# Two fixed tiles for the decay matrices, and a planner that knows transfers queue

## The chip, the cores and the metric

The kernel is one program on one NeuronCore of a Trainium2 chip. Five engines take part: TensorE (PE; its weight loads are listed as PEld), VectorE (DVE), ScalarE (ACT), GpSimd (POOL) and SyncE (SP), which does no arithmetic and issues every DMA of this program. The metric is device time in microseconds of one execution. Before the change the median of three runs is 2250.44 us (2250.43 to 2253.73). A program on one core has a single span; "clock" below is the share of TensorE's clock that the throttle granted, as the trace records it.

## What is computed

A two-layer decoder trunk on 1024 positions of width 1024, float32. Layer 0 is attention and a gated linear recurrence; the change does not touch it. Layer 1, the "odd layer", is a gated DeltaNet with 16 value heads that share 8 key heads. Cut to what matters:

```python
qkv, z, b_logit, a_logit = split(rms_norm(h) @ w_in)
q, k, v = split(silu(causal_conv4(qkv)));  q, k = l2_normalize(q), l2_normalize(k)
decay = exp(where(causal, gcum[:, None] - gcum[None, :], -inf))      # per head and chunk
lower = where(strict, (k*beta) @ k.T * decay, 0)
u, w  = triangular_solve(lower + I, [v*beta, k*beta*exp(gcum)])
step:   v_new = u - w @ S;  o = (q*exp(gcum)) @ S + (q @ k.T * decay) @ v_new
        S = S * exp(g_last) + k_tail.T @ v_new
out = h + (rms_norm(o) * silu(z)) @ w_out
```

followed by a final RMSNorm. `gcum` is the running sum of the log decay within a chunk.

## The kernel before, in words

**Tiling.** The odd layer works on 8 key heads `hh`, each with its two value heads `e`, and on 8 chunks `c` of 128 positions. Head `hh` goes through four kinds of work:

- *Projections* with short convolutions (`proj`, `conv`, `way_out`): float32 products split into three single-pass matmuls of 128x512 (`pk`, `pv`, `pq`, `oz` in the trace). They are most of TensorE's work and depend on nothing of the recurrence. Their weights come through `raww` tiles, which ACT and DVE cut into `w_hi` and `w_lo`.
- *Inversion* (`invert(hh)`): tile `L`, 16 blocks of 128x128, blocks 2c and 2c+1 for chunk c. `decays` loads the running sums of one chunk from the DRAM tile `gcd`, 128 KB for two blocks; ACT turns them into decays (a Relu per block with bias `g_ngc`, an Exp for four blocks); TensorE forms k k^T into the PSUM tile `kk` (four chunks a tile, so `kk{hh}_0` and `kk{hh}_1`, in one bank "c"); DVE multiplies it onto `L`. A long chain on DVE inverts 32x32 triangles, and three rounds of short matmuls join them (`qp` and `up`, 32x32, then `q2`/`u2`, 64x64). The result overwrites `L` and is called `U`.
- *Recurrence* (`recur(hh)`), chunk after chunk: `ks` and `qs` (state times k and q), `vp` (which reads U of this chunk), `kv`, `op`. The causal part needs a tile `A` per chunk, also loaded from `gcd` (128 KB), masked by POOL, passed through Exp on ACT and multiplied by `qk` on DVE.
- *Output* (`normed`, `gated`): POOL scales, TensorE transposes (`ot`), the result goes to DRAM.

**What runs beside what.** While `recur(hh)` runs, `invert(hh+1)`, the projections of head hh+1 and the output of head hh-1 are recorded as its filler. So the L of head hh+1 is needed at the start of stage hh, right where `recur(hh-1)` has just finished.

**What sets the order.** Nothing of the odd layer is issued when the Python code reaches it. `Plan` records all 8709 operations, finds their dependencies by overlapping elements (`edges`), and `run` sets them out in time by a list schedule: again and again it takes the engine that can start soonest and, of its operations that are ready, the one recorded earliest. `times` (line 119) says how long an operation holds its engine and when its result is there; it is a table of constants, for a DMA 430 ns of SP and 3100 ns to the landing, whatever else is in flight. `give` (line 291) then issues everything in the order of the planned starts, and each engine works strictly in that order. Hence nearly all instructions of this layer have line L291 in the profile, and groups are told apart by tile.

**Tiles that rotate.** `L` comes from a pool tag "L" with two buffers: a new tile takes the place of the tile before last, and both the planner (the "gates" in `edges`) and the framework make the first use of the new tile wait for *every* use of the old. The L of head hh+1 takes the buffer of head hh-1, which is read until the last `vp` of `recur(hh-1)`. The same tag also serves `gtmp` at the start of the layer and `g7` at its end. One operation waits for more than its data: the tile framework orders accesses to one PSUM tile, so a matmul into `kk` that stands behind a DVE read of the same tile in the issued order waits for that read.

Of the kernel before, what the change touches and what calls it, by code (L numbers as in the profile page):

```python
# [10 lines left out]
F32 = mybir.dt.float32  # L11
# [8 lines left out]
P = 128  # L20
D = 1024
T = 1024
NT = T // P
# [58 lines left out]
class Plan:  # L82
# [33 lines left out]
    def elems(ap):  # L116
        return int(np.prod([n for _, n in ap.ap[1:]], dtype=np.int64))

    def times(self, op, last):

        key, name, a, out = op["key"], op["name"], op["a"], op["out"][0]
        n = self.elems(out)
        if key == "SP":
            return 430, 3100
        if key == "PE":
            if name == "transpose":
                return 109, 290
            r32 = a[1].dtype == F32R
            rows, cols = a[2].ap[0][1], self.elems(a[1])
            small = rows < 128 or cols < 128  # L130
            if small:
                held = 28 if cols == 32 else 62
            else:
                held = n / 2.4 * (1 if r32 else 4) + (17 if r32 else 8)
            if small != last.get("small", False):
                held += 100
            last["small"] = small
            return held, held + 190
        if key == "DVE":
            if name == "transpose":  # L140
                t = 1980 if n >= 1024 else 1060 if out.ap[-1][0] != 1 or a[1].ap[-1][0] != 1 else 95 + 1.03 * n
            elif name == "memset":
                t = 60 + 0.86 * n
            elif n < 24:
                t = 82
            elif out.ap[0][1] == 32:
                t = 715
            elif n >= 512:
                t = (65 if name == "scalar_tensor_tensor" and len(op["ins"]) == 3 else 12) + 1.155 * n
            elif name == "scalar_tensor_tensor":  # L150
                t = 260
            else:
                t = 72 + 1.03 * n
            return t, t + 83
        if key == "ACT":
            if n < 24:
                t = 200
            elif op["ins"][0].space == PSUM:
                t = 249 if n <= 128 else 268 if n <= 256 else 0.93 * n
            else:  # L160
                t = 293 if n <= 128 else 307 if n <= 256 else 1.02 * n
            if n >= 512 and (len(op["ins"]) > 1 or out.ap[0][1] == 32):
                t += 100
            return t, t + (230 if "accum_out" in op["kw"] else 110)
        if name == "memset":
            return 565, 565
        t = 750 if n <= 256 or out.ap[0][1] == 32 else 1010 if len(op["ins"][1].ap) > 2 else 1250
        return t, t + 50
# [55 lines left out]
    def run(self):  # L224
        ops = self.ops
        pred, gates = self.dag = self.edges()
        n = len(ops)
        succ = [[] for _ in range(n + len(gates))]
        deg = [0] * (n + len(gates))
        for i, ps in enumerate(pred):  # L230
            for j in ps:
                succ[j].append(i)
                deg[i] += 1
        for g, (old, new, _) in enumerate(gates):
            inner = set(new)
            for j in old:
                succ[j].append(n + g)
                deg[n + g] += 1
            for i in new:
                if not pred[i] & inner:  # L240
                    succ[n + g].append(i)
                    deg[i] += 1
        keys = ("PE", "DVE", "ACT", "POOL", "SP")
        ready = {k: [] for k in keys}
        free = {k: 0.0 for k in keys}
        at = [0.0] * (n + len(gates))

        def release(j, done, key):
            for i in succ[j]:
                k = ops[i]["key"] if i < n else None  # L250
                if k is None:
                    t = done
                else:
                    t = 0.0 if k == key == "PE" else done + (self.OWN if k == key else self.SEM[k])
                at[i] = max(at[i], t)
                deg[i] -= 1
                if not deg[i]:
                    if i < n:
                        ready[k].append(i)
                    else:  # L260
                        release(i, at[i], None)

        for i in range(n):
            if not deg[i]:
                ready[ops[i]["key"]].append(i)
        last, starts, done_n, ends = {}, [0.0] * n, 0, [0.0] * n
        while done_n < n:
            best = None
            for k in keys:
                if ready[k]:  # L270
                    s = max(free[k], min(at[i] for i in ready[k]))
                    if best is None or s < best[0]:
                        best = s, k
            if best is None:
                raise RuntimeError("the order of the tiles' places does not work out")
            s, k = best
            i = min((i for i in ready[k] if at[i] <= s), key=lambda i: ops[i]["want"])
            ready[k].remove(i)
            held, got = self.times(ops[i], last)
            starts[i] = s  # L280
            free[k] = s + held
            ends[i] = s + got
            release(i, s + got, k)
            done_n += 1
        self.starts, self.ends = starts, ends
# [26 lines left out]
def trunk_kernel(ctx: ExitStack, tc: tile.TileContext, x, ew, ewo, ow, owab, owo, nw, fnw, lbl, hnw,  # L312
# [148 lines left out]
    def ab_half(w, half):  # L461

        w = w.rearrange("p (k j) -> p k j", k=KC)
        p = bank("pj", [P, 512], f"abp{half}")
        s = slice(half * 512, half * 512 + 512)
        for k in range(2):
            for r in range(4):
                for part in ("hi", "lo"):
                    pe.matmul(p[32 * r:32 * r + 32], w[:, 2 * r + k], hn(part, 2 * r + k, s).bitcast(F32),
                              start=k == 0 and part == "hi", stop=k == 1 and part == "lo")  # L470
        return p
# [605 lines left out]
    def odd_layer(es):  # L1077
        plan.ops = []
        sp = es.enter_context(tc.tile_pool(name="od", bufs=1))
        gt = {n: sp.tile([P, NT, 16], F32, name=f"g_{n}") for n in ("beta", "gc", "ngc", "eg", "nbeg", "etl", "egl")}  # L1080
        MA = sp.tile([P, 128], F32, name="MA")
        sync.dma_start(MA, cst[:, C_MA:C_MA + 128])
        cws = sp.tile([P, 32, 4], F32, name="cws")
# [5 lines left out]
        def gates():  # L1089
# [12 lines left out]
            for half in range(2):  # L1102
                p = begun.pop(("ab", half), None) or ab_half(w, half)
                s = slice(half * 512, half * 512 + 512)
# [6 lines left out]
            yield 3, 1.6  # L1111
            act.activation(gt["beta"], tp[:, :, 0:16], AF.Sigmoid)

            tmp = sp.tile([P, 6, NT, 16], F32, name="gtmp", tag="L", bufs=2)
            a_, u, w_, l_, d_, g = (tmp[:, i] for i in range(6))
            dve.tensor_tensor(a_, tp[:, :, 16:32], dt[:, None, :].to_broadcast([P, NT, 16]), op=ALU.add)
            dve.scalar_tensor_tensor(u, a_, -1.0, a_, op0=ALU.mult, op1=ALU.max)
            act.activation(u, u, AF.Exp, scale=-1.0)
# [69 lines left out]
        def turn_q(j):  # L1188
            CQ[j] = sp.tile([P, NT], F32, name=f"cq{j}", tag="cq", bufs=3)
            ss = sp.tile([P, NT], F32, name=f"qss{j}", tag="qss", bufs=2)  # L1190
            turn_qk(Q[j], ss, f"tq{j}")
            dve.tensor_scalar(CQ[j], ss, 4.0 * EPS, 128.0 * EPS, op0=ALU.add, op1=ALU.mult)
# [64 lines left out]
        G7 = []  # L1257
# [36 lines left out]
                yield from gate(hh, w, e, lambda h, g: gated(hh, e, h, g))  # L1294

        def gate7():
            G7.append(sp.tile([P, 2, 2, 512], F32, name="g7", tag="L", bufs=2))
            turn_q(7)
            w = unit()
            for e in range(2):  # L1300
                yield from gate(7, w, e, lambda h, g: None)
# [13 lines left out]
        def invert(hh):  # L1315
            kT = KT[hh]

            L = sp.tile([P, 16, 128], F32, name=f"L{hh}", tag="L", bufs=2)
            Lg = sp.tile([P, 16, 32], F32, name=f"Lg{hh}", tag="Lg")

            for c in range(0, NT, 2):

                decays(L[:, 2 * c:2 * c + 2, :], hh, c)
                decays(L[:, 2 * c + 2:2 * c + 4, :], hh, c + 1)
                for u in range(4):
                    act.activation(L[:, 2 * c + u, :], L[:, 2 * c + u, :], AF.Relu,
                                   bias=gt["ngc"][:, c + u // 2, 2 * hh + u % 2:2 * hh + u % 2 + 1])
                act.activation(L[:, 2 * c:2 * c + 4, :], L[:, 2 * c:2 * c + 4, :], AF.Exp, scale=-1.0)
            for h in range(2):
# [18 lines left out]
            for k in range(31):  # L1348
                n = k // 2 + 1
# [66 lines left out]
        def recur(hh):  # L1416
# [4 lines left out]
            def decay_a(c):  # L1421
                DA = sp.tile([P, 2, 128], F32, name=f"A{hh}_{c}", tag="A", bufs=4)
                decays(DA, hh, c)
                pool.tensor_tensor(DA, DA, MA[:, None, :].to_broadcast([P, 2, 128]), op=ALU.add)
                for e in range(2):
# [126 lines left out]
    with ExitStack() as es:  # L1552
        odd_layer(es)
# [65 lines left out]
```

## Time and profile before

| what | value |
|---|---|
| runs, median | 2250.44 us |
| profiled execution, its own time | 2252.19 us |
| its span, first to last instruction | 2250.4 us |
| mean granted clock of TensorE | 0.982 |
| busy in the span | PE 96%, PEld 79%, DVE 63%, ACT 42%, POOL 11% |
| chain that ended last | PE 82%, DVE 7%, DMA 6%, ACT 2%, issue 2%, SPq 1% |
| odd layer in the span | about 1204 us to the end |

"Busy" counts arithmetic; a PE that waits shows as idle before the instruction that ends the wait, with the releaser behind an arrow. A PE at half clock still counts as busy, so lost clock has to be read from the column PEclk of a table by stretches. "Issue" is a wait for nothing that the profile can name. SPq is SP's queue: an entry there that lasts longer than the usual 0.3 to 0.4 us is a DMA instruction that itself had to wait.

### The profile page before, as it was taken

The numbers are of one execution on the slowest core, as the hardware profiler recorded it, in microseconds if no ns is written. First come the engines' busy times: TensorE is split into PE (matmuls) and PEld (weight loads), VectorE is DVE, ScalarE is ACT, GpSimd is POOL, SyncE is SP. The second block draws the span as 40 slices with busy tenths as digits, with TensorE's granted clock in tenths as the row PEclk, the third lists the DMA queues.
The fourth block names the chain that finished last, engine by engine and source line by source line (L and its number), as shares of the span: only waits on it lengthen the run. The fifth ranks groups of instructions, "written<-read, shape, count | busy, mean of one in ns | idle before, by whom it ended". The sixth has DMA issues, their size and how long they took to land.

```text
span 2250.4 us, 52461 instructions
## 1 busy us (share of the span) xinstructions
PE 2159.4 (96%) x21781; PEld 1776.3 (79%) x21781; DVE 1417.3 (63%) x3236; ACT 945.3 (42%) x2519; POOL 247.3 (11%) x252
## 2 busy tenths in 40 slices
PE   7999999999999999989999898989999999999998
PEld 6888888888887878757887687868787787887887
DVE  6353535453444444457677896968788787965677
ACT  6233333333232223222236755655565555553223
POOL 0010101010000000000000012221212121220100
PEclk9999999999999999989999999989999999999999
DMA  4111111114333334353233413231212323224223
GB/s 148 39 49 48 44 48 47 45 39 121 98 99 90 108 98 131 92 165 99 88 118 110 78 40 52 77 64 57 74 53 68 60 67 54 78 74 145 94 95 121
DMA packets 100079, 184.15 MB, mean 82 GB/s; under 512 B 12672, under 2 KB 30208, under 8 KB 99840
## 3 DMA queue, kind: packets, MB, share of 16 engines
q1 hardware_dynamic: 99840, 180.79, 27.9%
q8 instruction: 171, 2.80, 0.5%
q14 instruction: 68, 0.56, 0.1%
HBM read 151.25 MB, written 29.49 MB: 80 GB/s over the span
## 4 chain that ended last, share of the span: by engine, by line
PE 82%; DVE 7%; DMA 6%; ACT 2%; issue 2%; SPq 1%; POOL 0%; DVEq 0%; ACTq 0%; POOLq 0%
PE op L291 8%; PE op L305 7%; PE oz L291 7%; PE pv L291 6%; PE avp L305 4%; PE bq L305 4%; PE ak L305 4%; PE aq L305 4%; PE ag L305 4%; PE bf L305 4%; PE bip L305 4%; PE bg L305 3%; PE pk L291 3%; PE o L305 3%; PE S L305 3%; DMA L<-gcd 2%
## 5 line engine op out<-in xcount | busy, mean ns | idle before, releaser
L305 DVE TENSOR_TENSOR w_lo<-raww,w_hi 128x512 fp32r<-128x512 f32 x168 | 123.4, 738 | 151.3 <-ACT w_hi L305 150.7
L305 ACT CAST w_hi<-raww 128x512 fp32r<-128x512 f32 x168 | 104.3, 621 | 217.3 <-DMA raww<-in_ewo_dram 56.9
L291 PE MATMUL op<-w_hi,yplo 128*128 128x512 f32 x448 | 140.2, 391 | 0.7 <-DVE hr L291 0.7
L305 ACT ACTIVATE P<-P,nm 128x256 f32<-128x256 f32 (+7 forms) x128 | 71.4, 559 | 135.4 <-DVE nm L305 135.2
L291 DVE TENSOR_TENSOR hr<-hr,op 128x512 f32<-128x512 f32 x128 | 87.4, 686 | 47.4 <-PE op L291 44.9
L305 PE MATMUL op<-w_hi,yphi 128*128 128x512 f32 x320 | 104.7, 401 | 10.1 <-DVE hres L305 9.7
L291 ACT CAST w_hi<-raww 128x512 fp32r<-128x512 f32 x124 | 76.3, 615 | 84.3 <-DMA raww<-in_owo_dram 37.2
L291 PE MATMUL oz<-hn_hi,w_hi 128*128 128x512 f32 x256 | 111.6, 436 | 0.0
L291 PE MATMUL pv<-hn_hi,w_hi 128*128 128x512 f32 x256 | 108.9, 425 | 1.0 <-ACT uv L291 1.0
L291 POOL TENSOR_TENSOR A<-A,MA 128x256 f32<-128x256 f32 x64 | 57.3, 897 | 461.1 <-DMA A<-gcd 226.5
L291 PE MATMUL oz<-hn_lo,w_hi 128*128 128x512 f32 x256 | 105.3, 411 | 0.0
L291 PE MATMUL oz<-hn_hi,w_lo 128*128 128x512 f32 x256 | 104.5, 408 | 0.0
L291 PE MATMUL pv<-hn_lo,w_hi 128*128 128x512 f32 x256 | 104.4, 408 | 0.0
L291 PE MATMUL pv<-hn_hi,w_lo 128*128 128x512 f32 x256 | 102.4, 400 | 0.0
L291 DVE TENSOR_TENSOR w_lo<-raww,w_hi 128x512 fp32r<-128x512 f32 x124 | 91.7, 742 | 16.0 <-ACT w_hi L291 13.8
L305 DVE STREAM_TRANSPOSE PB<-P 128x256 f32<-128x256 f32 (+3 forms) x64 | 54.6, 853 | 73.1 <-ACT P L305 73.1
L291 PEld LDWEIGHTS op<-w_hi,yplo 128*128 128x128 f32 x448 | 84.1, 188 | 18.3 <-DVE hr L291 0.9
L291 PE MATMUL op<-w_lo,yplo 128*128 128x512 f32 x224 | 87.2, 389 | 0.0
L305 DVE TENSOR_TENSOR hres<-hres,op 128x512 f32<-128x512 f32 x96 | 64.8, 682 | 30.3 <-PE op L305 29.4
L305 PEld LDWEIGHTS op<-w_hi,yphi 128*128 128x128 f32 x320 | 61.1, 191 | 25.6 <-DVE hres L305 11.4
L305 DVE CUSTOM_DVE_ANT_0 P<-S,G 128x256 f32<-128x256 f32 (+7 forms) x128 | 58.1, 492 | 36.8 <-PE S L305 36.4
L305 POOL TENSOR_TENSOR ay<-ay,sg 128x512 f32<-128x512 f32 x16 | 20.1, 1278 | 498.6 <-DMA ay<-rdd 498.6
(355 smaller groups left out, 6406.4 us busy)
## 6 DMA issues: line engine op xcount, KB each, us to landing
raww<-in_ew_dram SPq DMA_DIRECT2D x128, 256.0 KB, 3.0
raww<-in_ow_dram SPq DMA_DIRECT2D x100, 256.0 KB, 3.0
V<-vd SPq DMA_DIRECT2D x64, 256.0 KB, 5.2
rawy<-ymix SPq DMA_DIRECT2D x64, 256.0 KB, 2.7
raww<-in_ewo_dram SPq DMA_DIRECT2D x32, 256.0 KB, 3.0
L<-gcd SPq DMA_DIRECT2D x64, 128.0 KB, 9.4
A<-gcd SPq DMA_DIRECT2D x64, 128.0 KB, 2.9
ymix<-oy SPq DMA_DIRECT2D x32, 256.0 KB, 2.3
```

The costliest lines, as they stand in the source:

```text
L291: ops[i]["f"](*ops[i]["a"], **ops[i]["kw"])
L305: return f(*a, **kw)
```

## The change

Three things, all in the odd layer.

1. `L` no longer rotates. `LL` holds two fixed tiles of the same size for the whole layer; head hh uses `LL[hh % 2]`, `gtmp` becomes six blocks of `LL[1]`, and `g7` all of `LL[0]`. With no new tile there is no wait for a whole old one: each load of a chunk depends on the operations that touch the same elements, the last of them the `vp` of that chunk two heads earlier.
2. The planner's time to the landing of a DMA becomes the larger of 3000 ns and what brings it to 1250 ns behind the last planned landing.
3. `run` passes the start time to `times` and keeps the last planned landing.

The operations, their number and their sizes stay the same; the order in which the engines get them changes, since the planner decides it.

```diff
--- before.py
+++ after.py
@@ -116,12 +116,12 @@
     def elems(ap):
         return int(np.prod([n for _, n in ap.ap[1:]], dtype=np.int64))
 
-    def times(self, op, last):
+    def times(self, op, last, at=0.0):
 
         key, name, a, out = op["key"], op["name"], op["a"], op["out"][0]
         n = self.elems(out)
         if key == "SP":
-            return 430, 3100
+            return 430, max(3000, last.get("landed", 0) + 1250 - at)
         if key == "PE":
             if name == "transpose":
                 return 109, 290
@@ -276,7 +276,9 @@
             s, k = best
             i = min((i for i in ready[k] if at[i] <= s), key=lambda i: ops[i]["want"])
             ready[k].remove(i)
-            held, got = self.times(ops[i], last)
+            held, got = self.times(ops[i], last, s)
+            if k == "SP":
+                last["landed"] = s + got
             starts[i] = s
             free[k] = s + held
             ends[i] = s + got
@@ -1078,6 +1080,8 @@
         plan.ops = []
         sp = es.enter_context(tc.tile_pool(name="od", bufs=1))
         gt = {n: sp.tile([P, NT, 16], F32, name=f"g_{n}") for n in ("beta", "gc", "ngc", "eg", "nbeg", "etl", "egl")}
+
+        LL = [sp.tile([P, 16, 128], F32, name=f"L{i}") for i in range(2)]
         MA = sp.tile([P, 128], F32, name="MA")
         sync.dma_start(MA, cst[:, C_MA:C_MA + 128])
         cws = sp.tile([P, 32, 4], F32, name="cws")
@@ -1111,8 +1115,7 @@
             yield 3, 1.6
             act.activation(gt["beta"], tp[:, :, 0:16], AF.Sigmoid)
 
-            tmp = sp.tile([P, 6, NT, 16], F32, name="gtmp", tag="L", bufs=2)
-            a_, u, w_, l_, d_, g = (tmp[:, i] for i in range(6))
+            a_, u, w_, l_, d_, g = (LL[1][:, i].rearrange("p (c h) -> p c h", c=NT) for i in range(6))
             dve.tensor_tensor(a_, tp[:, :, 16:32], dt[:, None, :].to_broadcast([P, NT, 16]), op=ALU.add)
             dve.scalar_tensor_tensor(u, a_, -1.0, a_, op0=ALU.mult, op1=ALU.max)
             act.activation(u, u, AF.Exp, scale=-1.0)
@@ -1294,7 +1297,7 @@
                 yield from gate(hh, w, e, lambda h, g: gated(hh, e, h, g))
 
         def gate7():
-            G7.append(sp.tile([P, 2, 2, 512], F32, name="g7", tag="L", bufs=2))
+            G7.append(LL[0].rearrange("p (e h u) n -> p e h (u n)", e=2, h=2))
             turn_q(7)
             w = unit()
             for e in range(2):
@@ -1315,7 +1318,7 @@
         def invert(hh):
             kT = KT[hh]
 
-            L = sp.tile([P, 16, 128], F32, name=f"L{hh}", tag="L", bufs=2)
+            L = LL[hh % 2]
             Lg = sp.tile([P, 16, 32], F32, name=f"Lg{hh}", tag="Lg")
 
             for c in range(0, NT, 2):
```

How the order moves is shown at three places. First SP, around the loads of L for head 4 (`L4` before, `LL[0]`, printed as `L0`, after), before:

```order
L291 DMA A2_7_15134<-gcd_14303 128x256
L291 DMA raww52_1_15147<-in_ow_dram 128x512
L291 DMA A3_0_15186<-gcd_14303 128x256
L291 DMA raww52_2_15150<-in_ow_dram 128x512
L291 DMA Tp4_15249<-in_cst_dram 128x512
L291 DMA A3_1_15205<-gcd_14303 128x256
L291 DMA raww52_3_15153<-in_ow_dram 128x512
L291 DMA raww53_0_15194<-in_ow_dram 128x512
L291 DMA A3_2_15218<-gcd_14303 128x256
L291 DMA raww53_1_15197<-in_ow_dram 128x512
L291 DMA raww53_2_15200<-in_ow_dram 128x512
L291 DMA L4_15187<-gcd_14303 128x256 x8
```

and now, the same stretch of SP's queue:

```order
L293 DMA L0_14314<-gcd_14303 128x256
L293 DMA A2_7_15131<-gcd_14303 128x256
L293 DMA L0_14314<-gcd_14303 128x256
L293 DMA raww52_1_15144<-in_ow_dram 128x512
L293 DMA A3_0_15183<-gcd_14303 128x256
L293 DMA raww52_2_15147<-in_ow_dram 128x512
L293 DMA L0_14314<-gcd_14303 128x256
L293 DMA Tp4_15245<-in_cst_dram 128x512
L293 DMA A3_1_15201<-gcd_14303 128x256
L293 DMA raww52_3_15150<-in_ow_dram 128x512
L293 DMA raww53_0_15190<-in_ow_dram 128x512
L293 DMA L0_14314<-gcd_14303 128x256
```

Eight loads in a row at the end of the stage have become eight single ones; four of them stand here, three stood ahead of this stretch, and the last one comes four places behind it.

Second, ACT at the same boundary. `pq3_0` and `pq3_1` are the two halves of head 3's q projection, `uq3` and `q3` the tiles of its convolution. Before:

```order
L291 COPY uq3_15174<-pq3_0_15175 128x512
L291 ACTIVATE L4_15187<-L4_15187,g_ngc_14309 128x128
L291 ACTIVATE q3_15183<-uq3_15174,cws_14315 128x512
L291 ACTIVATE L4_15187<-L4_15187,g_ngc_14309 128x128 x2
L291 ACTIVATE L4_15187<-L4_15187 128x512
L291 ACTIVATE L4_15187<-L4_15187,g_ngc_14309 128x128 x4
L291 ACTIVATE L4_15187<-L4_15187 128x512
L291 ACTIVATE L4_15187<-L4_15187,g_ngc_14309 128x128
L291 ACTIVATE uq3_15174<-q3_15183 128x512
L291 ACTIVATE L4_15187<-L4_15187,g_ngc_14309 128x128 x3
```

and now:

```order
L293 ACTIVATE L0_14314<-L0_14314,g_ngc_14309 128x128
L293 COPY uq3_15171<-pq3_0_15172 128x512
L293 ACTIVATE L0_14314<-L0_14314,g_ngc_14309 128x128
L293 ACTIVATE q3_15180<-uq3_15171,cws_14317 128x512
L293 ACTIVATE L0_14314<-L0_14314 128x512
L293 ACTIVATE A3_3_15235<-A3_3_15235,g_ngc_14309 128x128 x2
L293 CAST w53_hi1_15191<-raww53_1_15193 128x512
L293 ACTIVATE uq3_15171<-q3_15180 128x512
L293 CAST w53_hi2_15194<-raww53_2_15196 128x512
```

Between the two activations of `q3`'s convolution (the scaling and the Tanh) ACT had nine operations on L; now one is left, and work that used to stand behind them (`A3_3`, two casts of weights) has come forward.

Third, TensorE at the start of the layer, around the second k k^T tile of head 0. `pv0_0_1` is a half projection of 24 matmuls, `tk1` the transposes of head 1's k. Before, `kk0_1` stood after its eighth matmul:

```order
L291 MATMUL pv0_0_1_14381<-hn_hi0_13908,w42_hi2_14263 128x512
L291 MATMUL pv0_0_1_14381<-hn_lo0_13910,w42_hi2_14263 128x512
L291 MATMUL kk0_1_14364<-kT0_14320 128x128 x4
L291 MATMUL pv0_0_1_14381<-hn_hi0_13908,w42_lo2_14264 128x512
L291 MATMUL pv0_0_1_14381<-hn_hi0_13908,w42_hi2_14263 128x512
```

and now behind all 24:

```order
L293 MATMUL pv0_0_1_14381<-hn_hi1_13909,w42_hi3_14269 128x512
L293 MATMUL pv0_0_1_14381<-hn_lo1_13911,w42_hi3_14269 128x512
L293 MATMUL pv0_0_1_14381<-hn_hi1_13909,w42_lo3_14270 128x512
L293 MATMUL kk0_1_14364<-kT0_14322 128x128 x4
L293 MATMUL tk1_0_14366<-ident_69,kT1_14358 128x128 x4
```

So `kk0_1` moved 16 matmuls of 128x512 later. From the second half of stage 2 on, TensorE's order at the boundaries (around `kk4` to `kk7`) is the same as before.

## The prediction

> **What bounds the kernel now.** I read the page first, then the waits of TensorE over the odd layer (1200 to 2250 us), then the timeline at each wait over 1 us, then tables by stretches for the clock.
>
> ```profile
> PE 2159.4 (96%) x21781; PEld 1776.3 (79%) x21781; DVE 1417.3 (63%) x3236; ACT 945.3 (42%) x2519; POOL 247.3 (11%) x252
> q8 instruction: 171, 2.80, 0.5%
> L<-gcd SPq DMA_DIRECT2D x64, 128.0 KB, 9.4
> A<-gcd SPq DMA_DIRECT2D x64, 128.0 KB, 2.9
> ...
> PE kk L291 <- DVE L L291: 21.8, 13, 4.0
> PE pq L291 <- issue: 8.6, 1, 8.6
> ```
>
> TensorE sets the time: it is busy 96% of the span, so time comes back only where it stands still or runs at half clock. Its largest waits in the odd layer belong to `kk`, which waits for DVE's products on `L` (21.8 us in 13 waits, up to 4.0). A transfer of 128 KB lands 2.9 us after its issue when it is `A`, and 9.4 us when it is `L`: same size and source, but `L` comes eight at once.
>
> The timeline at the boundary of stages 2 and 3 shows how that reaches TensorE:
>
> ```profile
> 1568.90 3.94 SPq L291 DMA_DIRECT2D raww<-in_ow_dram  x2
> 1573.19 4.54 SPq L291 DMA_DIRECT2D L<-gcd  x8
> 1583.51 0.69 ACT L291 ACTIVATE L<-L,g_ngc 128x128 f32<-128x128 f32 x2 [1.44 <-DMA L<-gcd]
> 1586.68 0.61 ACT L291 ACTIVATE uq<-q 128x512 f32<-128x512 f32 x1
> 1587.32 0.69 DVE L291 SCALAR_TENSOR_TENSOR q<-uq,q 128x512 f32<-128x512 f32 x1 [4.06 <-ACT uq L291]
> 1588.33 0.80 PE L291 MATMUL kk<-kT 128*128 128x128 f32 x2 [3.55 <-DVE L L291]
> 1591.59 0.61 ACT L291 CAST w_hi<-raww 128x512 fp32r<-128x512 f32 x1
> 1600.97 0.49 PE L291 MATMUL kk<-kT 128*128 128x128 f32 x2 [0.45 <-DVE L L291]
> ```
>
> ACT stands in its queue for landings of `L`, and the Tanh of q's convolution (1586.68) stands behind them; DVE has waited 4.06 us for that Tanh, its first product on `L` stands behind q, and the last matmul of the first `kk` tile waits 3.55 us for that product. The second `kk` tile, 12 us on, meets a landed `L` and waits 0.45 us: that is what such a tile costs without a late load. The same pattern comes at the next three boundaries, at two of them with a second wait a little later:
>
> ```profile
> 1693.53 0.79 PE L291 MATMUL kk<-kT 128*128 128x128 f32 x2 [3.89 <-DVE L L291]
> 1799.06 0.80 PE L291 MATMUL kk<-kT 128*128 128x128 f32 x2 [3.97 <-DVE L L291]
> 1809.36 0.71 PE L291 MATMUL vp<-bv,L 128*128 128x128 f32 x4 [2.30 <-DVE A L291]
> 1904.90 0.79 PE L291 MATMUL kk<-kT 128*128 128x128 f32 x2 [3.65 <-DVE L L291]
> 1914.99 0.71 PE L291 MATMUL vp<-bv,L 128*128 128x128 f32 x4 [2.08 <-DVE A L291]
> ```
>
> A wait also costs clock. By stretches, from the end of a wait to the end of the half-clock record (the third column from the end is the granted clock), and behind them two pieces of the chain of waits:
>
> ```profile
> 1243.31:1248.98 5.67, 5.67 (x14) 4.55 (x15) 4.59 (x12) 4.89 (x11) 0.73 (x1) 0.50 0.74 163
> 1382.10:1385.50 3.40, 3.40 (x48) 2.67 (x38) 1.05 (x4) 1.91 (x5) 0.00 (x0) 0.50 1.02 68
> 1389.48:1395.75 6.27, 6.27 (x39) 4.45 (x41) 1.10 (x2) 2.44 (x6) 4.22 (x4) 0.50 0.00 0
> 1475.71:1484.50 8.79, 8.79 (x47) 6.31 (x47) 2.16 (x6) 2.68 (x6) 3.03 (x3) 0.50 0.02 4
> 1588.33:1593.73 5.40, 5.40 (x14) 4.34 (x15) 4.24 (x10) 4.93 (x12) 2.16 (x2) 0.50 0.14 43
> 1693.53:1699.54 6.01, 6.01 (x17) 4.85 (x17) 4.83 (x10) 5.51 (x14) 3.97 (x4) 0.50 0.10 36
> 1799.06:1801.94 2.88, 2.88 (x8) 2.40 (x9) 1.64 (x6) 2.31 (x6) 0.05 (x1) 0.50 0.52 88
> 1904.90:1907.75 2.85, 2.85 (x8) 2.37 (x9) 1.64 (x6) 1.80 (x5) 0.37 (x1) 0.50 0.51 86
> 1809.50:1813.00 3.50, 3.06 (x19) 2.62 (x20) 1.77 (x5) 0.37 (x1) 1.28 (x1) 1.00 0.25 83
> ...
> 1589.13 4.94 PE oz L291 x12
> 1988.40 2.75 PE pq L291 x12
> ```
>
> Behind each wait of 3.5 us or more stand 2.9 to 8.8 us at half clock; behind the wait of 2.30 us (1809.50) the clock is 1.00. Twelve matmuls take 4.94 us at half clock and 2.75 us otherwise, so I count half of such a stretch as lost.
>
> **The sum.** It is made against the span, 2250.4 us, which is also the median of the runs (2250.44); the profiled execution's own time, 2252.19, has 1.8 us around the span that no edit touches.
>
> *The four steady boundaries.* The loads leave the boundary, each behind the `vp` that frees its chunk, some 13 us apart (a stage of 105.5 us, by the last row of this part, has eight). By then most of `L` is landed and decayed; only the last chunk, which the second `kk` tile needs 12 us later, loads at the boundary itself. ACT's Tanh has one operation on `L` ahead of it, so DVE's product follows q at once. TensorE's order there is the same, so what goes is the excess of the wait over 0.45 us: 3.55 + 3.89 + 3.97 + 3.65 = 15.06, less 4 x 0.45, is 13.3 us. With a wait of 0.45 us the clock stays up: half of 5.40 + 6.01 + 2.88 + 2.85 = 17.14 is 8.6 us. The waits of 2.30 and 2.08 us for DVE's `A` come from the same backlog; with DVE no longer late I leave 0.3 us of each, and take 3.8 of the 4.4. Together **25.7 us**.
>
> *The burst for head 3.* TensorE waits 8.64 us for "issue":
>
> ```profile
> 1475.71 0.80 PE L291 MATMUL pq<-hn_lo,w_hi 128*128 128x512 f32 x1 [8.64 <-issue]
> 1458.70:1476.00 17.30, 8.66 (x192) 6.70 (x192) 11.16 (x24) 8.28 (x22) 4.16 (x6) 0.85 0.81 84
> 1678.00:1695.10 17.10, 13.21 (x66) 11.01 (x65) 9.85 (x27) 9.49 (x26) 0.00 (x0) 0.93 0.27 84
> ```
>
> The page counts 171 instruction transfers, and TensorE's 2 x 21781 instructions make 255 to a transfer. During this burst it went through 384 (the short `qp` and `up`), in the same time at a later boundary through 131. So here it needed new instructions while the DMA engines were 0.81 busy with `L`; I read the wait as a late instruction transfer. Without a burst there is nothing to be late behind: 8.64 + half of 8.79 = 13.0 us, of which I take **12**. [...]
>
> *The burst for head 2.*
>
> ```profile
> 1380.50 0.22 PE L291 MATMUL up<-Q,Tn 32*32 32x32 f32 x2 [1.08 <-DVE Q L291]
> 1389.48 0.69 PE L291 MATMUL ot<-ident,bv 128*128 128x128 f32 x2 [3.63 <-POOL bv L291]
> ```
>
> 4.7 us of waits and half of 3.40 + 6.27, 4.8 us, make 9.5; the `ot` waits for POOL, which has its `A` from a load behind the burst. The order here is laid out anew, so I take three quarters, **7**.
>
> *The start.* Both `L0` and `L1` still come as bursts, since nothing holds their tiles back.
>
> ```profile
> 1240.85 0.94 PE L291 MATMUL kk<-kT 128*128 128x128 f32 x6 [2.08 <-DVE L L291]
> 1243.31 0.79 PE L291 MATMUL kk<-kT 128*128 128x128 f32 x2 [1.52 <-DVE L L291]
> 1252.92 0.66 PE L291 MATMUL tk<-ident,kT 128*128 128x128 f32 x4 [2.37 <-DVE kT L291]
> ```
>
> `kk0_1` moves 16 projection matmuls later, 3.7 us at 2.75 us for twelve, which covers the 2.08 + 1.52 us of its waits; with half of the 5.67 us of clock that is 6.4 us. The 2.37 us would make it 8.8. As the bursts stay and still block ACT, I take **4.5**.
>
> *New waits.* Head 0's recurrence begins 23 matmuls later, and ACT now meets a landing at eight places of a stage instead of one. A lone 128 KB landing (2.9 us) keeps the planned 3.0, so most will be in time. Bounds: nothing, or two new waits like that of `ot` with their clock, 2 x (3.6 + 1.7) = 10.6 us; I take **5**, one of them.
>
> 25.7 + 12 + 7 + 4.5 - 5 = 44.2: **2206 us**. DVE does not become the bound:
>
> ```profile
> 1688.80:1794.30 105.50, 100.91 (x700) 84.12 (x699) 87.96 (x225) 60.08 (x178) 21.96 (x23) 0.97 0.25 63
> ```
>
> in a stage that shrinks from 105.5 to 99 us it still works 88.
>
> **The rivals.** (1) *The "issue" wait is no late transfer* and stays: 2206 + 12 = 2218 us. For it: only one such wait in the layer is long, while six bursts pass with less. Against: it has the most instructions and the longest half clock. (2) *The wait passes to q*: DVE is 83% busy in a stage, and the product on `L` stands behind all of q's convolution. If the `kk` waits shrink only to half, they stay near 2 us; and if then neither the clock nor the two `vp` waits get better, the boundaries give 7.5 instead of 25.7: 2224 us. Against: DVE's 4.06 us before q were idle. (3) *SP is blocked* (the slower end). Each of eight loads of `L` now waits in SP's one queue for the `vp` that frees its chunk, and the weights and `A` stand behind it.
>
> ```profile
> SPq L291 <- PE qk L291: 213.5, 50, 12.3
> ```
>
> SP already waits like this, 4.3 us on average and up to 12.3, and TensorE waits for no weights. Two weight tiles went out from 1568.90 on and the cast came at 1591.59, some 19 us after the landing. It decides from a hold beyond 19 us; with holds of 30 us in six stages the loss is 6 x 11 = 66 against 44 gained: 2272 us. (4) *The order moves and the time does not*: the chunk that loads last at the boundary holds the first `kk` as long as eight did: 2250 us. Against: the first `kk` reads the four chunks that are freed first.
>
> **How the numbers follow.** Forecast 0.66, rival 1 0.15, rival 2 0.12, rival 3 0.04, rival 4 0.03. What a measurement can tell from no change is about 0.2%, 4.5 us. Forecast and rivals 1 and 2 are faster by more: 0.93; same 0.03; slower 0.04. All terms in full and no new wait: 25.7 + 13.0 + 9.5 + 8.8 = 57.0, which is 2193 us, the lower end. Upwards the range takes in both faster rivals, the 5.6 us by which the bound of new waits exceeds my 5, and 2 us for the runs: 2232.
>
> **What would show it.** `L<-gcd` lands in 3 to 4 us at the median instead of 9.4. The first `kk` wait of heads 4 to 7 is near 0.45 us, with no half clock behind it. No "issue" wait over 2 us between 1440 and 1500 us. `vp` no longer waits over 1 us for `A` at two boundaries. The step from one `kk` boundary to the next is 99 to 100 us. The forecast is wrong if the `kk` waits stay above 1.5 us with `L` landed (rival 2), if the 8.64 us reappear (rival 1), or if ACT's `w_hi` begins to hold TensorE (rival 3).

## The result, and the profile after

The changed kernel takes **2191.99 us** (median of four runs, 2190.66 to 2193.18) against 2252.09 us before: a ratio of 0.973, 95% interval 0.9714 to 0.9747. The span of the profiled execution is 2188.8 us (2250.4 before), the mean granted clock 0.995 (0.982). The forecast was 2206 us with a range of 2193 to 2232: the sign was right and the mechanism in part, the time lies 1 us under the lower end, and the gain is 60 us where 44 were forecast.

From the page of the changed kernel, TensorE's busy time and the landings of the two kinds of decay loads:

```profile
PE 2138.4 (98%) x21781; PEld 1762.1 (81%) x21781; DVE 1405.6 (64%) x3236; ACT 944.5 (43%) x2518; POOL 238.4 (11%) x252
...
L<-gcd SPq DMA_DIRECT2D x64, 128.0 KB, 2.9
A<-gcd SPq DMA_DIRECT2D x64, 128.0 KB, 2.9
```

`L` now lands as fast as `A` (2.9 us at the median, 9.4 before). The matmul `kk` that waited 3.55 to 3.97 us at each of the four steady boundaries, in the timeline of the changed kernel:

```profile
1556.22 0.49 PE L293 MATMUL kk<-kT 128*128 128x128 f32 x2 [0.44 <-DVE L L293]
...
1556.78 0.39 PE L293 MATMUL oz<-hn_lo,w_hi 128*128 128x512 f32 x1
...
1655.33 0.49 PE L293 MATMUL kk<-kT 128*128 128x128 f32 x2 [0.44 <-DVE L L293]
...
1754.49 0.49 PE L293 MATMUL kk<-kT 128*128 128x128 f32 x2 [0.45 <-DVE L L293]
...
1853.66 0.49 PE L293 MATMUL kk<-kT 128*128 128x128 f32 x2 [0.44 <-DVE L L293]
```

The waits are 0.44 us, the projection matmuls behind them take 0.39 us (full clock), and the step from one of these matmuls to the next is 99.1 to 99.2 us (105.2 to 105.8 before).

**Where the time came from.** Tables by stretches, cut so that before and after begin with the same number of matmuls done: the start of the layer with heads 0 and 1, the burst for head 2, the burst for head 3, the steady boundaries, and the end. Columns: from, to, length, then the busy time of PE (count), PEld, DVE, ACT and POOL, granted clock, DMA share, GB/s. Before:

```profile
1189.00:1307.00 118.00, 108.56 (x692) 83.38 (x691) 93.61 (x237) 81.42 (x212) 9.26 (x11) 0.97 0.38 87
1307.00:1445.50 138.50, 130.99 (x911) 107.40 (x910) 114.03 (x330) 79.39 (x238) 27.55 (x29) 0.96 0.25 56
1445.50:1546.50 101.00, 91.36 (x703) 74.53 (x701) 82.22 (x237) 55.78 (x174) 25.07 (x29) 0.93 0.30 64
1546.50:1968.30 421.80, 399.68 (x2855) 333.19 (x2856) 350.24 (x898) 239.24 (x699) 88.81 (x92) 0.98 0.25 64
1968.30:2250.40 282.10, 270.04 (x1345) 223.05 (x1334) 187.34 (x337) 95.76 (x231) 25.55 (x23) 0.99 0.31 105
...
2064.34:2068.18 3.84, 3.64 (x10) 2.87 (x11) 2.24 (x5) 1.60 (x3) 0.00 (x0) 0.56 0.43 137
```

After:

```profile
1187.90:1303.60 115.70, 111.68 (x692) 85.34 (x692) 94.76 (x241) 81.10 (x214) 8.69 (x11) 1.00 0.36 90
1303.60:1429.10 125.50, 121.26 (x927) 101.34 (x917) 113.60 (x323) 81.95 (x245) 24.41 (x29) 1.00 0.23 66
1429.10:1517.70 88.60, 86.96 (x698) 72.28 (x698) 80.82 (x240) 57.27 (x180) 22.57 (x27) 1.00 0.27 74
1517.70:1915.00 397.30, 392.10 (x2863) 327.25 (x2858) 342.30 (x901) 234.90 (x684) 86.22 (x95) 1.00 0.22 66
1915.00:2188.80 273.80, 266.39 (x1351) 220.40 (x1339) 185.59 (x335) 95.65 (x230) 25.49 (x23) 0.99 0.31 109
```

Since the order moved, a plain difference of lengths mixes in work that changed places between neighbours (short matmuls against long ones). What was lost in a stretch is its idle time (length less PE busy) and half of what ran at half clock (an estimate, as in the prediction: twelve matmuls took 4.94 us there and 2.75 us otherwise). By that count the gain is:

| stretch | idle before, after | half clock, halved | gain | forecast |
|---|---|---|---|---|
| start | 9.44, 4.02 | 2.8 | 8.2 | 4.5 |
| burst for head 2 | 7.51, 4.24 | 4.8 | 8.1 | 7 |
| burst for head 3 | 9.64, 1.64 | 4.4 | 12.4 | 12 |
| four boundaries | 22.12, 5.20 | 8.6 | 25.5 | 25.7 |
| end | 12.06, 7.41 | 1.7 | 6.3 | none |
| new waits | | | in the rows above | -5 |
| sum | | | 60.5 | 44.2 |

The half-clock column is taken from the stretches that the prediction lists; at the end it is the row at 2064.34, of which 3.4 us ran at half clock. The spans differ by 61.6 us; the other 1.1 lie ahead of 1189 us, in a part that no edit touches. The one long wait of the layer that the prediction did not look into is in the end stretch, and the last experiments are about it.

### The profile page after: what moved, and what is told of

It reads as the page before. It is cut to its first block, busy times and chain, and to the rows that moved or that the text cites. A ratio compares the mean times of both kernels' runs of the same rounds, so it can differ in the third digit from the quotient of the medians.

```text
span 2188.8 us, 52451 instructions
## 1 busy us (share of the span) xinstructions
PE 2138.4 (98%) x21781; PEld 1762.1 (81%) x21781; DVE 1405.6 (64%) x3236; ACT 944.5 (43%) x2518; POOL 238.4 (11%) x252
## 4 chain that ended last, share of the span: by engine, by line
PE 83%; DVE 10%; DMA 3%; ACT 3%; issue 1%; SPq 0%; DVEq 0%; ACTq 0%
PE op L293 9%; PE oz L293 7%; PE op L307 7%; PE avp L307 4%; PE bq L307 4%; PE aq L307 4%; PE ak L307 4%; PE pv L293 4%; PE ag L307 4%; PE bf L307 4%; PE bip L307 4%; PE bg L307 3%; PE pk L293 3%; PE o L307 3%; PE pq L293 3%; PE S L307 3%
## 5 line engine op out<-in xcount | busy, mean ns | idle before, releaser
L307 DVE TENSOR_TENSOR w_lo<-raww,w_hi 128x512 fp32r<-128x512 f32 x168 | 123.4, 738 | 151.9 <-ACT w_hi L307 151.3
L293 DVE TENSOR_TENSOR w_lo<-raww,w_hi 128x512 fp32r<-128x512 f32 x124 | 87.0, 703 | 17.1 <-ACT w_hi L293 14.7
L293 DVE SCALAR_TENSOR_TENSOR vT<-uv,cws,vT 128x512 f32<-128x512 f32 x96 | 73.6, 767 | 8.2 <-ACT vT L293 7.2
```

The costliest lines, as they stand in the source:

```text
L293: ops[i]["f"](*ops[i]["a"], **ops[i]["kw"])
L307: return f(*a, **kw)
```

## The experiments

The theory after the result, called A below: late landings of `L` make the boundaries, a late instruction transfer makes the wait in head 3's burst, and the planner's order alone makes the gain at the start and at the end. The rivals were that the planner's order carries the boundaries too, that the "issue" wait is no late transfer, and that TensorE need not have waited for `L` at all. In the table below, the same count as above (idle and half clock against before, in us; negative is gained) is made for each kernel:

| kernel | start | head 2 | head 3 | boundaries | end |
|---|---|---|---|---|---|
| the change | -8.3 | -8.1 | -12.4 | -25.5 | -6.2 |
| fixed tiles alone | 1.2 | -10.2 | -13.3 | -25.6 | 2.1 |
| planner alone | -7.6 | -6.3 | -2.5 | -16.3 | -6.2 |
| before, instructions shifted | 0.4 | -0.1 | -10.5 | 4.6 | 0.2 |
| before, kk released | 0.6 | -1.1 | -3.0 | 4.8 | 2.1 |
| before, hr spaced | -0.5 | -0.5 | -2.3 | 1.4 | -6.4 |
| change, hr not spaced | -8.2 | -7.9 | -12.4 | -25.4 | 0.1 |
| change, kk released | -8.2 | -8.7 | -13.0 | -29.3 | -6.1 |

Each row is one execution. The kernel "before, hr spaced" gives the engines the order of before up to 2045 us, and its first four columns still differ from zero by 0.5 to 2.3 us: that much, two executions of the same order differ.

**The fixed tiles alone.**

```diff
-            return 430, max(3000, last.get("landed", 0) + 1250 - at)
+            return 430, 3100
```

> The change with the planner's old landing of a fixed 3100 ns: the two fixed tiles alone. Its order has single loads of L from head 2 on, one operation on L ahead of ACT's Tanh at a boundary, kk0_1 where it stood before, and at the end ACT's casts of rawy ahead of oq7_5 as before. Theory A (fixed tiles spread the loads; boundaries 24.5, head 2 8.8, head 3 15.7 us, counted from the two traces at equal numbers of matmuls; the start's 3.4 and the end's 7.2 belong to the planner): 2252 - 49 = 2203 us, the kk waits of heads 4 to 7 at 0.45 us, no wait for issue over 2 us near 1475, and a wait of about 4 us for oq7_5 with half clock behind it at the end. Rival B (most of the order comes from the planner's landings, and the tiles alone earn about half): 2225 us, with some kk waits above 1.5 us. Rival C (the end's wait does not hang on the order of ACT and goes as well): 2196 us.

Measured: 2204.17 us, ratio 0.9788 (0.9773 to 0.9803). Theory A was right to 1 us. From the landings of its page and its waits of TensorE in the odd layer:

```profile
L<-gcd SPq DMA_DIRECT2D x64, 128.0 KB, 3.1
...
PE kk L293 <- DVE L L293: 8.6, 13, 2.7
PE vp L293 <- ACT oq L293: 4.8, 1, 4.8
PE tk L293 <- DVE kT L293: 3.0, 1, 3.0
```

`L` is spread without any help of the planner; all of heads 2 and 3 and of the boundaries is there. The start's waits (`tk`, and 3.7 us of the `kk` in two waits) and the wait for `oq` at the end stay.

**The planner alone.**

```diff
-        LL = [sp.tile([P, 16, 128], F32, name=f"L{i}") for i in range(2)]
...
-            L = LL[hh % 2]
+            L = sp.tile([P, 16, 128], F32, name=f"L{hh}", tag="L", bufs=2)
```

> The kernel before with the planner's new landings alone; the tiles of L still rotate, so L still comes eight loads at once, and six or seven operations on L still stand ahead of ACT's Tanh. At the end ACT's casts of rawy now stand behind oq7_5 and vn7_5, and kk0_1 stands later at the start. Theory A (the bursts make the boundaries' waits, the order makes the start's and the end's): the end gives 7.2 and the start 3.4 us, the boundaries nothing: 2252 - 10.6 = 2241 us, L<-gcd still lands in 9 us or more at the median, the kk waits of heads 4 to 7 stay over 3 us. Rival B (the planner's order carries the boundaries too): 2215 to 2225 us, kk waits near 0.5 us in spite of the bursts. The wait for issue in head 3's burst stays near 8.6 us if nothing moves the place of the instruction transfer.

Measured: 2213.93 us, ratio 0.9832 (0.9815 to 0.9849). Rival B was nearer, and theory A fell for the boundaries. `L` still comes eight at once and lands as late as before, but the waits at the four boundaries fall from 3.55 to 3.97 us to 1.33 to 1.96. From the page and the timeline, one boundary (the loads on SP, ACT's work, TensorE):

```profile
L<-gcd SPq DMA_DIRECT2D x64, 128.0 KB, 9.2
...
1658.43 6.18 SPq L293 DMA_DIRECT2D L<-gcd  x8
...
1669.43 0.69 ACT L293 ACTIVATE L<-L,g_ngc 128x128 f32<-128x128 f32 x2 [0.26 <-DMA L<-gcd]
1670.03 0.61 ACT L293 ACTIVATE uq<-q 128x512 f32<-128x512 f32 x1
...
1673.10 0.40 ACT L293 ACTIVATE L<-L,g_ngc 128x128 f32<-128x128 f32 x1 [1.25 <-DMA L<-gcd]
...
1671.98 0.49 PE L293 MATMUL kk<-kT 128*128 128x128 f32 x2 [1.96 <-DVE L L293]
```

With the landings spaced in its plan, the list schedule lets the Tanh of q (1670.03) go ahead of the operations on the last pieces of `L`, which would only have stood waiting (1673.10). So about two thirds of the boundaries' loss (16.3 of 25.5 us) was not the late landing as such: it was that ACT, by its order, waited for landings with other engines' work behind it. The two halves of the change do not add up (48.3 + 38.6 us alone, 60 together), because either of them brings most of the boundaries and of head 2.

**Is the "issue" wait a late instruction transfer?** The kernel before with 32 tiny matmuls more, at the very start, where TensorE's first matmul begins at 8.64 us. On the page they are 64 matmuls and 64 weight loads (x21845 of each, x21781 before); if the transfers carry TensorE's instructions one after the other, every later one then comes some 128 instructions earlier in the work.

```diff
+    wz = cp.tile([P, 64], F32, name="wz")
+    dve.memset(wz, 0.0)
+    wps = bank("c", [P, 16, 32], "wps")
+    for u in range(16):
+        for r in (0, 64):
+            pe.matmul(wps[r:r + 32, u, :], wz[32 + r:64 + r, 0:32], wz[32 + r:64 + r, 32:64], start=True, stop=True)
```

> The kernel before with 32 tiny matmuls (32x32) more at the program's start, where TensorE waits for its first data for 8.7 us: some 128 TensorE instructions, about half of one instruction transfer, so that every later transfer is asked for about 128 instructions earlier in the work. The bursts of L are untouched. Theory A (the 8.64 us wait for issue is an instruction transfer that stands behind the burst): the wait at 1475 goes or shrinks below 3 us, with the half clock behind it; 2252 - 12 = 2240 us, if no other transfer falls into a burst. Rival 1 (the wait is no late transfer): it stays within 1 us of 8.64, and the time at 2252 us.

Measured: 2246.08 us, ratio 0.9972 (0.9962 to 0.9982). The 8.64 us are down to one microsecond, with the burst of `L` as it was (9.4 us to landing at the median of the page, as before):

```profile
1474.72 0.33 PE L291 MATMUL u<-Q,T 64*64 64x64 f32 x5 [1.05 <-issue]
```

The DMA queues by stretches show the transfer itself. The kernel before, from 1446 to 1472.5 us and from 1472.5 to 1475.7 us:

```profile
q1 hardware_dynamic: 1575, 1.70, 53.4%
q14 instruction: 2, 0.02, 0.2%
...
q1 hardware_dynamic: 434, 0.51, 83.0%
q8 instruction: 1, 0.02, 3.0%
```

For 26.5 us no packet of q8 moves; the next comes in the 3.2 us before TensorE goes on at 1475.71. In the shifted kernel it is there as the burst begins (1457.7 to 1460 us):

```profile
q1 hardware_dynamic: 118, 0.11, 17.3%
q8 instruction: 1, 0.02, 2.6%
```

The planner-alone kernel, whose burst is untouched, keeps the wait (7.98 us, with one q8 packet in the last 3.2 us before its end and none in the 16 us before).

Counting instructions shows where the wait stands. This is the row of the kernel before from its start to 1467.07 us, where TensorE stops:

```profile
0.00:1467.07 1467.07, 1419.77 (x17153) 1162.43 (x17153) 818.88 (x1836) 567.26 (x1458) 113.56 (x116) 0.99 0.29 83
```

17,153 matmuls and as many weight loads are 34,306 instructions, two more than 134 x 256. The three other kernels with this wait (planner alone, kk released, hr spaced) stop after 34,304 or 34,306 too, in two of them at other work (`up` where it is `pq` here), and the 1.05 us of the shifted kernel stand after 34,561, one more than 135 x 256. The page of before gives 255 of TensorE's 43,562 instructions to each of the 171 packets of q8; from that and these counts I estimate that what a packet had brought was used up at these places, though no trace shows what a packet holds. At the three multiples of 256 before, the q8 packet began 0.5 and 0.1 us after TensorE's passing and 0.9 us ahead of it; at the two before those, in head 2's burst, 6.5 and 6.1 us after it. TensorE passed the next one, 34,048, at 1462.31 us, and the packet began at 1473.04: 10.7 us later, 6 us after TensorE had stopped. In the changed kernel, which has no burst there, it began 1.4 us after the same multiple, and TensorE did not wait. So rival 1 is out: TensorE went on 2.7 us after this packet began, and I read the wait as an instruction transfer that came late behind the burst. When it was asked for is not in the trace, so what held it up stays open.

Head 3 gains 10.5 us; the time gains only 6.4, because the boundaries lose 4.6 of it (`kk` now waits 4.70 us at the first of them). Why they are longer there I did not find out.

**Need TensorE wait for late L at all?** The fourth `kk` matmul of a tile stands behind DVE's first read of that tile and so waits for DVE, which in turn waits for `L`. One number of the planner puts it ahead.

```diff
-            return held, held + 190
+            return held, held + (300 if out.tensor.name.startswith("kk") else 190)
```

> The kernel before with one number of the planner: a kk matmul counts as done 300 ns after its end in place of 190. So the fourth kk matmul of a tile stands ahead of DVE's first product in program order and does not wait for DVE; loads, tiles and ACT's order at the boundaries are as before. Theory A (L is late for the work that follows too: the wait passes from kk to the next matmul that needs DVE, a vp or the short qp): the four boundaries keep two thirds or more of their 24.5 us, 2244 us or more. Rival D (TensorE waited for late L only because that one matmul stands behind the product; it has enough other work until L is needed): kk waits of heads 4 to 7 vanish and nothing comes in their place, 2252 - 22 = 2230 us or less, with L<-gcd still at 9 us.

Measured: 2254.66 us, ratio 1.0011 (1.0000 to 1.0022): nothing gained. The wait passes on. One boundary in the timeline:

```profile
1694.29 0.44 PE L291 MATMUL ot<-ident,bv 128*128 128x128 f32 x2 [0.97 <-POOL bv L291]
...
1700.11 1.22 PE L291 MATMUL vp<-bv,L 128*128 128x128 f32 x4 [3.94 <-DVE A L291]
```

POOL and DVE are as late as before, and the next matmuls that need them wait instead. Rival D is out, theory A holds for this.

**The same edit on the changed kernel**, where ten waits of 0.44 us at `kk` are left.

> The change with one number of the planner more: a kk matmul counts as done 300 ns after its end in place of 190, so that the fourth kk matmul of heads 2 to 7 stands ahead of DVE's first product and does not wait for it. In the changed kernel ten such waits of 0.44 us are left. Theory A (with L landed in time nothing stands behind them): ten waits gone, 2192 - 4.4 = 2187.6 us. Rival (as in the run with the same edit on the kernel before, the wait passes to the next matmul that needs DVE or POOL, here an ot or a vp): 2192 us, with new waits of 0.4 us at ot or vp.

Measured: 2184.80 us, ratio to before 0.9708 (0.9685 to 0.9732). To compare it with the change itself, both were run again on one chip:

> The change itself again, beside the other two of this call: 2192 us.

> The change with kk matmuls counted as done 300 ns after their end, on the same chip as the change itself. 2185 us, 7 us below the change, if the gain of the earlier run holds; above 2188 us if it was that chip's.

Measured: the change 2193.64 us (2192.03 to 2194.81), with the edit 2185.80 us (2185.69 to 2187.94); ratios to before 0.9736 (0.9713 to 0.9758) and 0.9704 (0.9681 to 0.9726). It beats both kernels, by 7.8 us against the change. The waits of TensorE in the odd layer, first of the change, then with the edit:

```profile
PE kk L293 <- DVE L L293: 6.2, 11, 1.7
```

```profile
PE kk L293 <- DVE L L293: 1.6, 1, 1.6
```

The same edit is worth nothing where DVE is late and 7.8 us where it is in time: 4.6 us of waits at `kk`, and the short waits of `ks` in the recurrence, 2.4 us in all, went too.

**A longer spacing.** In bursts `L` lands some 1.9 us apart (the eight loads issued from 1678.06 us on landed from 1681.63 to 1695.10 us in the kernel before, 1.92 us a step), the change plans with 1.25.

```diff
-            return 430, max(3000, last.get("landed", 0) + 1250 - at)
+            return 430, max(3000, last.get("landed", 0) + 1900 - at)
```

> The change with 1900 ns between planned landings in place of 1250; 1.9 us is what lies between two landings of L in a burst (1686.74, 1688.79, 1690.73 in the trace of before). Theory A (what is left at the start, 1.69 us at kk0_1 and 1.11 at tv, comes from landings later than planned): about 3 us less, 2189 us. Rival (a spacing that is too long for single loads moves work back that could go earlier): 2192 us or more, with new waits elsewhere.

> The change with both numbers: kk matmuls done at 300 ns, and 1900 ns between planned landings. If both theories A hold, 2192 - 4.4 - 2.8 = 2185 us; if the two edits disturb each other, between 2187 and 2193 us.

Measured: 2192.59 us (ratio 0.9742, 0.9719 to 0.9765), and with the `kk` edit 2186.19 us (0.9714, 0.9691 to 0.9737). The rival was right: the wait at `kk0_1` goes, but a `kk` that waits 2.1 us for DVE's `kT` and longer waits of `tv` (2.4 us in all, 1.6 in the change) take its place. The second time lies between its two forecasts and decides nothing. Of these two spacings neither is the faster; no other was run.

**The end, which the prediction had not counted.** The kernel before, in the timeline: SP's loads, ACT, and TensorE.

```profile
2048.24 5.27 SPq L291 DMA_DIRECT2D hr<-h  x8
2053.62 1.02 SPq L291 DMA_DIRECT2D rawy<-ymix  x2
...
2062.51 1.25 ACT L291 CAST yplo<-rawy 128x512 fp32r<-128x512 f32 x2 [6.18 <-DMA rawy<-ymix]
2063.67 0.62 ACT L291 ACTIVATE oq<-qs,g_eg 128x128 f32<-128x128 f32 x2
...
2064.34 0.49 PE L291 MATMUL vp<-r,L 128*128 128x128 f32 x2 [3.97 <-ACT oq L291]
```

Two pieces of `rawy` (256 KB each) queue behind eight loads of `hr` (512 KB each) and land 8.9 us after their issue; the median of all `rawy` loads is 2.7. ACT stands 6.18 us at their casts, `oq` of head 7's chunk 5 stands behind them, and `vp` behind that. In the changed kernel the loads are the same, and the casts come last:

```profile
1993.20 5.23 SPq L293 DMA_DIRECT2D hr<-h  x8
1998.53 1.13 SPq L293 DMA_DIRECT2D rawy<-ymix  x2
...
2002.62 0.63 ACT L293 ACTIVATE oq<-qs,g_eg 128x128 f32<-128x128 f32 x2 [1.33 <-PE qs L293]
...
2007.76 1.26 ACT L293 CAST yplo<-rawy 128x512 fp32r<-128x512 f32 x2 [1.53 <-DMA rawy<-ymix]
```

Two kernels move these casts alone, the first on the kernel before, the second on the change:

```diff
+            if out.tensor.name.startswith(("hr", "rawy")):
+                got = max(3000, last.get("landed", 0) + 1250 - at)
+                last["landed"] = at + got
+                return 430, got
             return 430, 3100
```

> The kernel before with the planner's spaced landings for the transfers of hr alone (the eight 512 KB loads and rawy's pieces keep their order of issue; every other transfer, L too, keeps 3100 ns). On ACT the two last casts of yplo9 move behind oq_5 and vn_5 of head 7; up to there the order is that of the kernel before. Theory A (the wait of 3.97 us at 2064 and its half clock come from those two casts standing in front of oq_5 while rawy lands 9 us late): that wait goes, 2252 - 7 = 2245 us, and all waits before 2050 us stay as they were. Rival (rawy's lateness passes to the output projection that reads yplo9): 2250 us or more, with a wait at op of 3 us or more.

```diff
-            return 430, max(3000, last.get("landed", 0) + 1250 - at)
+            return 430, 3100 if out.tensor.name.startswith(("hr", "rawy")) else max(3000, last.get("landed", 0) + 1250 - at)
```

> The change with the old fixed landing of 3100 ns for the transfers of hr alone. Up to 2000 us its order is that of the change; on ACT the two last casts of yplo9 stand again in front of oq_5 and vn_5 of head 7, as in the kernel before. Theory A (the part of the gain that the prediction did not count comes from the place of these two casts): a wait of 4 to 5 us at vp for oq with 3 to 7 us of half clock comes back, and the time is 7 us above the change's, 2199 us. Rival (the tail's gain comes from the calmer transfers ahead of it): it stays at 2192 us, without that wait.

Measured: 2246.27 us (ratio 0.9976, 0.9961 to 0.9991), 4.7 us under before, and 2199.92 us (0.9762, 0.9739 to 0.9784), 6.3 us above the change on the same chip (2193.64). In the first the wait is gone; in the second it is back, with the same chain:

```profile
2012.62 1.25 ACT L293 CAST yplo<-rawy 128x512 fp32r<-128x512 f32 x2 [6.25 <-DMA rawy<-ymix]
2013.77 0.62 ACT L293 ACTIVATE oq<-qs,g_eg 128x128 f32<-128x128 f32 x2
...
2014.44 0.49 PE L293 MATMUL vp<-r,L 128*128 128x128 f32 x2 [4.04 <-ACT oq L293]
```

Moved both ways, two casts are worth 5 to 6 us: this part of the gain is shown to be the planner's, and has nothing to do with `L`.

## Why the prediction was right and where it failed

- *What bounds the kernel, and rivals 2, 3 and 4*: right. The `kk` waits fell to 0.44 us, the waits of `vp` for `A` over 1 us are gone, and no wait of TensorE's in the layer goes back to weights.
- *The four steady boundaries*, 25.7 us: measured 25.5. The mechanism is shown, since the fixed tiles alone bring 25.6. But the burst is not the only thing that can be changed: the planner alone removes 16.3 us with the bursts in place. That the sum fits to 0.2 us is partly luck: four waits of `vp` for `A` went, 4.9 us, where 3.8 us of two were counted, and 1.6 us of new short waits stand against it.
- *The burst for head 3*, 12 us: measured 12.4, and the shifted kernel bears out the cause, a late instruction transfer: its wait is 1.05 us instead of 8.64.
- *The burst for head 2*, 7 us: measured 8.1, a difference within what two executions of the same order differ.
- *The start*, 4.5 us: measured 8.2. The step that failed is the halving, "as the bursts stay and still block ACT". The bursts do stay (eight loads of `L` in a row from 1225.66 and from 1236.36 us in the changed kernel), but the kernel with the planner alone gains 7.6 there: as at the boundaries, the new order takes the waits away in spite of the bursts. Which engine's order does it at the start, no run separates.
- *New waits*, -5 us. The step that failed is to deduct one wait like that of `ot`, 3.6 us with 1.7 of clock: none of that kind came. What came is short and costs no clock: `q` for ACT's `L` (2.5 us in four waits, 0.6 in one before), `ks` (2.2 us in five, none before), `u` (0.8, 0.2 before) and `tq` (0.6): some 5 us more than before, and none over 1.0. They are already taken off in the rows of the table, which reach the forecast even so.
- *Not in the sum*: the wait of 3.97 us at 2064 us and its half clock, 6.3 us. It stands as the fourth line in the view of TensorE's waits that the prediction read:

```profile
PE vp L291 <- ACT oq L291: 4.0, 1, 4.0
```

Only waits around `L` were followed to their cause, though the edit to the planner concerns every transfer. This is the step that took the time out of the range: its lower end adds up all terms in full, 57.0 us, but no term for the end.

The three failed steps make 3.7 + 5 + 6.3 = 15 of the 16 us that were missing. Two of them, the start and the end (10 us), come from one error: the change was costed as "L is spread", and its second half, a planner that knows that transfers queue, as a detail. The deduction is another matter: with the fixed tiles alone no such wait came either.

## What to carry to other kernels

When one edit changes a cost in a scheduler, list every long wait of the profile and ask of each whether that cost orders it, not only those that the edit's other half is about. Here a late transfer cost little by itself: with the planner alone `L` still landed 9.2 us after its issue, and 16.3 of the boundaries' 25.5 us were gone. What cost was the work behind the instruction that waited for it, so a better place in the order can be worth much of what an earlier landing is. Taking away a wait paid only where the engine behind it was in time: the same edit brought nothing before this change and 7.8 us after it.

## What was not expected of the hardware

An instruction transfer of TensorE's came late behind a burst of data loads here: 8.64, 7.98, 7.9 and 8.3 us of waiting in four kernels with that burst (before, planner alone, kk released, hr spaced), and 1.05 us when the instruction stream was shifted by 128 instructions. So adding instructions that do no useful work made the kernel 6.4 us faster (2252.48 to 2246.08 us).

Of two waits, of 1.89 and 2.30 us, the shorter was followed by half clock, the longer was not. The planner-alone kernel at one more boundary, and rows of 3.41 us each, the first three of this kernel (the first holds 1.67 us of the wait of 1.96 us shown earlier), the last two of the kernel before, around its wait of 2.30 us:

```profile
1874.69 0.49 PE L293 MATMUL kk<-kT 128*128 128x128 f32 x2 [1.89 <-DVE L L293]
...
1670.31:1673.72 3.41, 1.74 (x9) 1.48 (x10) 2.52 (x10) 2.16 (x6) 1.98 (x2) 1.00 0.22 68
1871.70:1875.11 3.41, 1.52 (x11) 1.25 (x11) 2.34 (x8) 2.43 (x6) 0.66 (x1) 1.00 1.02 73
1875.11:1878.52 3.41, 3.41 (x10) 2.64 (x9) 2.77 (x7) 2.89 (x7) 3.38 (x4) 0.50 0.97 119
...
1805.36:1808.77 3.41, 1.70 (x10) 1.20 (x8) 3.41 (x3) 1.21 (x3) 3.07 (x3) 1.00 0.24 77
1808.77:1812.18 3.41, 2.75 (x16) 2.32 (x16) 2.18 (x7) 0.86 (x2) 1.28 (x1) 1.00 0.24 77
```

In the traces of the kernel before and of the change every stretch at half clock in the span (12 and 3) begins a whole number of steps of 3.413 us after the first of its trace, within 0.02 us, and lasts one, two or four of them (3.41, 6.83, 13.65 us), but for the last (6.75 and 5.46 us), in which the span ends. In their odd layer the half clock goes with TensorE's idle time within one such step: the ten steps at full clock with 2.13 us idle or more were followed by half clock, none with less than 1.70 us was, and in between 1.70 us was followed by it, 1.71 and 1.85 us were not. Ahead of that layer it is less clear: 1.46 us was followed by it once (the step at 973.71 us of the change). Short waits counted together once: ahead of the half clock at 1382.10, 1.70 us were idle in the step, the longest single wait being 1.08 us.

The wait of 1.89 us lies in one row whole, and the next row runs at 0.50. Of the waits of 1.96 and 2.30 us, 1.67 and 1.71 us lie in the row of 1.00 that holds most of them, and the row behind the second shows 1.00 too. The steps lie elsewhere in the two executions (3.12 and 0.91 us from the span's start to the first of them), so, as I read it, the clock behind a wait of about 2 us is a matter of luck, and the prediction's reading, that half clock stands behind waits of 3.5 us or more, is too simple: 1.89 us was enough in the row above.
